# Weighted sums of four modulation rows: pairs behind fixed VectorE operations in place of bursts of eight, and a higher rank for two kinds of splits

## The chip, the cores and the metric

The kernel runs on one core of a Trainium2 chip. The metric is the device time of one execution in microseconds (us). The engines are TensorE (PE in the rows; PEld is its weight load), VectorE (DVE), ScalarE (ACT), GpSimd (POOL) and SyncE (SP), which issues most transfers. Each engine works through a queue of its own in order, and waits on semaphores for the others.

## What is computed

One layer of a diffusion backbone over 1024 latent tokens and 256 context tokens, model width 1024, all in 32-bit floats. Cut to what matters here:

```python
mod = silu(c) @ w_mod + b_mod                      # w_mod: 1024 x 6144
sh1, sc1, g1, sh2, sc2, g2 = split(mod, 6)         # six rows of 1024
hx = rmsnorm(x) * (1 + sc1) + sh1
proj = hx @ w_in                                   # u_f (512), u_x (512), u_g (512)
y_f = fft2(u_f).real                               # 4 groups of 128 channels
xc = dwconv(u_x, 4 taps)
for d in (0, 1):                                   # forward, backward
    r = sigmoid(xc @ wa[d]); i = sigmoid(xc @ wi[d])
    a = exp(-8 * r * softplus(-lam[d]))
    h = scan(a, sqrt(1 - a * a) * i * xc)
    y += h
y_r = y * gelu(u_g)
x = x + g1 * (concat(y_f, y_r) @ w_out)
hx2 = rmsnorm(x) * (1 + sc2) + sh2
out = rmsnorm(x + g2 * expert_choice_swiglu(hx2))  # 16 experts, d_ff 2816
```

The rows sh1 and sc1 are wanted at the start, and g1, sh2, sc2 and g2 only behind the mixing. The change concerns those last four.

## The kernel before

The program runs in stages. The first loads x and the context, makes sh1 and sc1, normalises and transposes (to about 75 us). `phase_c`, the mixing stage, follows up to about 270 us: the projections in tiles of 128 channels by 1024 tokens, the convolution, the gates and scans, the gelu product and the Fourier transform by matrices. `phase_f` multiplies by w_out (tiles mx) and adds the residual, to about 400 us. Then come the router and the 16 experts, up to the end.

TensorE computes in 32 bits by splitting both operands into a high and a low half and issuing three matmuls for each product (`mm3`, L611). For every weight tile ScalarE makes the high half (L227; `wh`) and VectorE the low half (L228; `wl`). The tiles of the projection are numbered ct: 0 to 3 give the Fourier input (`uf0` to `uf3`, PSUM), 4 to 7 the scan input (`ux`), 8 to 11 the gelu input (`ug0` to `ug3`). `get(ct)` loads a tile's two halves by h and calls `get_w` for both, so `wl8_0` is the low half of the first half of tile 8, which `ug0` reads. One projection is 48 matmuls of 512 columns.

For each t in 0 to 3 the stage computes: `conv(t)` (six multiply-adds, L658, tile xc), `xsplit(t)` (xch, xcl), four gate products on TensorE (`g`, 9 matmuls each; g201 is tile 2, direction 0, gate 1), sigmoids on ScalarE, the exponent and the square root there, the product with xc on VectorE (`lru_sig`, L697 to L700), `lru_scan` for each direction (two steps, L713 and L714, on tile r; the scan, L716, into tile g), the sum of both directions (L813), `gelu(t)` (product at L822, tile gg), `fourier_a(g)` (ScalarE copies the reversed half of uf to uT; VectorE makes tile U by L885 to L888). `fb_dft`, `fb_split`, `fb_trig` and `fb_evac` are the two matrix steps of the Fourier transform (tiles ab and abx, abl and xl, pq, T and yf). The projection outputs share two PSUM slots, so ug2 takes the slot of uf2 when VectorE has read it.

The weighted sums: `mod_acc(r, h)` makes half of modulation row r for all partitions. It loads w_mod in four transfers of 512 KB on GpSimd's queue (tile `mraw`, two buffers) and adds eight products of 128x512 into a tile `macc` on VectorE (L837 starts a sum, L839 adds). The tile is stored to `accd`; the matrix stage sums it over the partitions later. Eight calls of `mod_acc` are written by hand between the steps of `phase_c`.

The order on an engine is not that of the code: a scheduler sorts the instructions by priority, which follows the place in the program. `high_priority(offset=n)` moves an instruction ahead by n, and `pin` keeps an instruction behind the one traced before it on the same engine. Before, `get_w` and `fb_split` use the offset HP = 50, and `mod_acc` pins nothing.

Of the kernel before, what the change touches and what calls it, by code (L numbers as in the profile page):

```python
# [9 lines left out]
F32 = mybir.dt.float32  # L10
# [4 lines left out]
ALU = mybir.AluOpType  # L15

D = 1024
N = 1024
NCTX = 256
L = N + NCTX  # L20
KD = 8
# [138 lines left out]


class Kern:
    HP, HT, LATE = 50, 300, -100
    PAD = 32

    def __init__(self, ctx, tc, a, out, dbg=None):
# [429 lines left out]

    def get_w(self, ct, h):
        raw = self.wraw.pop((ct, h))
        with self.tc.high_priority(offset=self.HP):
            return self._get_w(ct, h, raw)  # L600

    def _get_w(self, ct, h, raw, pin=False, eng=None):
# [46 lines left out]
    def conv(self, t):  # L649
        nc = self.nc  # L650
        u = self.u.pop(t)
        xc = self.c5(f"xc{t}", tag="xc")
        col = lambda i: self.cols[:, COL["cw"] + 4 * i + t:COL["cw"] + 4 * i + t + 1]
        cb = self.cols[:, COL["cb"] + t:COL["cb"] + t + 1]
        for o, n, q in ((0, N, NCTX), (N, NCTX, 0)):
            nc.scalar.activation(xc[:, q:q + n], u[:, o:o + n], AF.Identity, scale=col(1), bias=cb)
            for i, a, b in ((0, 1, n), (2, 0, n - 1), (3, 0, n - 2)):
                nc.vector.scalar_tensor_tensor(xc[:, q + a:q + b], u[:, o + a + i - 1:o + b + i - 1], col(i),  # L658
                                               xc[:, q + a:q + b], op0=ALU.mult, op1=ALU.add)
        self.xc[t] = xc  # L660

    def xsplit(self, t):
# [47 lines left out]

    def lru_scan(self, d, r, g, a):
        V = self.nc.vector
        V.scalar_tensor_tensor(r, a, 1.0, r, op0=ALU.add, op1=ALU.mult)  # L713
        V.tensor_tensor(r, r, g, op=ALU.mult)  # L714
        s = slice(None) if d == 0 else slice(None, None, -1)
        V.tensor_tensor_scan(g[:, s], a[:, s], r[:, s], 0.0, op0=ALU.mult, op1=ALU.add)  # L716

    def phase_c(self, stop=None):
        nc = self.nc
        self.xc, self.xs, self.graw, self.gw = {}, {}, {}, {}  # L720
        self.ysp = self.dram.tile([7, 128, N], F32, name="ysp")
        self.yl = {}
        self.accd = self.dram.tile([4, 2, 128, 512], F32, name="accd")
        st = {}
        self.load_gate(0)
        self.conv(0)
        self.xsplit(0)
        self.load_trig()
        self.ux(2)
        self.gate_w(0)  # L730
        self.get(7)
        st[0] = self.lru_front(0)
        self.load_gate(1)
        self.conv(1)
        self.xsplit(1)
        self.ux(3)
        self.get(0)
        self.gate_w(1)
        self.lru_back(0, *st[0])
        self.fourier_a(0)  # L740
        self.mod_acc(0, 0)
        self.conv(2)
        self.get(8)
        self.load_gate(2)
        st[1] = self.lru_front(1)
        self.mod_acc(0, 1)
        self.xsplit(2)
        self.gelu(0)
        self.mod_acc(1, 0)
        self.gate_w(2)  # L750
        self.get(1)
        self.lru_back(1, *st[1])
        self.conv(3)
        self.fourier_a(1)
        self.mod_acc(1, 1)
        self.get(9)
        self.load_gate(3)
        st[2] = self.lru_front(2)
        self.mod_acc(2, 0)
        self.xsplit(3)  # L760
        self.gelu(1)
        self.mod_acc(2, 1)
        self.gate_w(3)
        self.get(2)
        self.lru_back(2, *st[2])
        self.fourier_a(2)
        self.mod_acc(3, 0)
        self.get(3)
        st[3] = self.lru_front(3)
        self.fourier_a(3)  # L770
        self.get(10)
        self.lru_back(3, *st[3])
        self.gelu(2)
        self.get(11)
        self.fd = {}
        self.fb_dft(0)
        self.fb_split(0)
        self.gelu(3)
        self.mod_acc(3, 1)
        if stop == "e":  # L780
            self.fd = {}
            for g in range(CT):
                self.fb_dft(g)
                self.fb_split(g)
                self.fb_trig(g)
                self.fb_evac(g)
# [21 lines left out]
    def lru_back(self, t, st, a):  # L808
        nc = self.nc
        for d in range(2):  # L810
            self.lru_scan(d, *st[d], a[d])
        g0, g1 = st[0][1], st[1][1]
        nc.vector.tensor_tensor(g0[:, NCTX:], g0[:, NCTX:], g1[:, 0:N], op=ALU.add)  # L813
        self.yl[t] = g0[:, NCTX:]

    def gelu(self, t):
        nc = self.nc
        p = self.p2(f"ug{t}")
        self.proj(p, 8 + t)
        gg = self.pr.tile([128, N], F32, tag="gg", name=f"gg{t}", bufs=1)  # L820
        nc.scalar.activation(gg, p, AF.Gelu_apprx_tanh)
        nc.vector.tensor_tensor(gg, gg, self.yl.pop(t), op=ALU.mult)  # L822
        self.dump(f"yr{t}", gg)
        nc.sync.dma_start(self.ysp[3 + t], gg)

    def mod_acc(self, r, h):
        nc, a = self.nc, self.a
        m, s = (2, 4, 3, 5)[r], slice(512 * h, 512 * h + 512)
        acc = self.pr.tile([128, 512], F32, tag="ht", name=f"macc{m}{h}", bufs=2)
        for kp in range(KD // 2):  # L830
            w = self.pro.tile([128, 2, 512], F32, tag="mraw", name=f"mraw{m}{h}{kp}", bufs=2)
            nc.gpsimd.dma_start(w, a["wmod"][m, 2 * kp:2 * kp + 2, :, s].rearrange("k p c -> p k c"))
            for i in range(2):
                k = 2 * kp + i
                c = self.cond[:, k:k + 1]
                if k == 0:
                    nc.vector.tensor_scalar(acc, w[:, i], c, None, op0=ALU.mult)  # L837
                else:
                    nc.vector.scalar_tensor_tensor(acc, w[:, i], c, acc, op0=ALU.mult, op1=ALU.add)  # L839
        nc.gpsimd.dma_start(self.accd[r, h], acc)  # L840

    def mod_row(self, r, acc, b, ones, p):
        nc = self.nc
# [32 lines left out]
    def fourier_a(self, g):  # L876
        nc = self.nc
        V = nc.vector
        p = self.p2(f"uf{g}")
        self.proj(p, g)  # L880
        U = self.c4(f"U{g}", (128, 2, 512))
        uT = self.pr.tile([128, 512], F32, tag="uT", name=f"uT{g}", bufs=1)
        nc.scalar.activation(uT, p[:, 1023:511:-1], AF.Copy)
        rev = uT[:, 0:511]
        V.tensor_tensor(U[:, 0, 1:], p[:, 1:512], rev, op=ALU.add)  # L885
        V.tensor_tensor(U[:, 1, 1:], p[:, 1:512], rev, op=ALU.subtract)
        V.tensor_copy(U[:, 0, 0:1], p[:, 0:1])
        V.tensor_copy(U[:, 1, 0:1], uT[:, 511:512])  # L888
        self.fo[g] = U
# [16 lines left out]
    def fb_split(self, g):  # L906
        p, px = self.fd[g]
        hi, lo = self.c4(f"abh{g}", (128, 8, 128), F32R), self.c4(f"abl{g}", (128, 8, 128), F32R)
        xh = self.pr.tile([1, 128], F32R, tag="xh", name=f"xh{g}", bufs=1)
        xl = self.pr.tile([1, 128], F32R, tag="xl", name=f"xl{g}", bufs=1)  # L910
        with self.tc.high_priority(offset=self.HP):
            for s in range(2):
                self.split(p[:, 512 * s:512 * s + 512].rearrange("p (a b) -> p a b", b=128),
                           hi[:, 4 * s:4 * s + 4], lo[:, 4 * s:4 * s + 4])
            self.split(px[0:1, 0:128], xh, xl)
        self.fd[g] = hi, lo, xh, xl
# [657 lines left out]
    def load(self, p):  # L1574
        if p >= len(self.order):
            return
        k, m = self.order[p]
        if k == "w":
            self.raws[m] = self.raw_tile(f"raw{m}")
            self.nc.sync.dma_start(self.raws[m], self.S[m][5])  # L1580
        else:
            src = self.accx.rearrange("(t p) c -> p t c", p=128)
            self.fin.append(self.raw_tile(f"fin{m}"))
            self.nc.sync.dma_start(self.fin[-1].rearrange("p (t c) -> p t c", t=2), src[:, 2 * m:2 * m + 2])
# [252 lines left out]
```

## Time and profile before

| what | value |
|---|---|
| median of 3 runs | 1981.69 us (1981.35 to 1982.66) |
| the profiled execution, own time | 1983.2 us |
| its span in the profile | 1981.4 us |
| TensorE busy | 1899.9 us |
| VectorE busy | 1750.4 us |
| ScalarE busy | 1357.3 us |
| accumulations | 8 of L837, 56 of L839 |
| transfers of mraw | 32, of 512 KB |

The span is the time between the first and the last recorded instruction of one execution. Busy times include the issue of neighbouring instructions that overlap by some hundredths of a us, so distances from start to start are used where a sum is made. A row of the timeline gives the start, the busy time, the engine, the line and operation, the tile written and the tiles read, and in brackets how long the engine sat idle before it and what released it.

### The profile page before, as it was taken

How to read it: one execution, taken by the hardware profiler on the slowest of the kernel's cores; microseconds unless marked ns; L12 is line 12 of the kernel's file. 1: busy time of each engine (PE TensorE's matmuls, PEld its weight loads, DVE VectorE, ACT ScalarE, POOL GpSimd, SP SyncE). 2: the span in 40 equal slices, each digit the busy share in tenths (PEclk: the TensorE clock that was granted, in tenths of full speed). 3: DMA queues.
4: the chain of work that ended last, by engine and by line, in shares of the span. 5: the costliest groups of instructions: out<-in, count | busy, mean ns of one | idle time of the engine just before them, and what ended most of it. 6: DMA issues, size and time to landing. Idle time of an engine off the chain costs nothing.

```text
span 1981.4 us, 24505 instructions
## 1 busy us (share of the span) xinstructions
PE 1899.9 (96%) x9434; PEld 1559.9 (79%) x9434; DVE 1750.4 (88%) x1629; ACT 1357.3 (69%) x1094; POOL 137.0 (7%) x134
## 2 busy tenths in 40 slices
PE   7989889969999999999999999999999999999996
PEld 2777777857787888888888888888888888888885
DVE  7889787789998989898999999998989898989897
ACT  6567643346676777777777777777777777777775
POOL 2310101220002000000000000000000000000000
PEclk9999989979999999999999999999999999999998
DMA  8353554578999999999999999999999999999994
GB/s 330 112 159 123 191 173 149 207 285 334 350 357 339 379 368 390 381 386 367 388 363 391 355 406 364 396 366 381 379 381 375 384 381 376 385 375 387 366 390 178
DMA packets 113956, 651.34 MB, mean 329 GB/s; under 512 B 12743, under 2 KB 20472, under 8 KB 46254
## 3 DMA queue, kind: packets, MB, share of 16 engines
q1 hardware_dynamic: 100718, 602.55, 79.2%
q0 software_dynamic: 10816, 38.82, 6.9%
q10 hardware_dynamic: 2304, 8.39, 1.1%
q8 instruction: 74, 1.21, 0.2%
q14 instruction: 44, 0.36, 0.0%
HBM read 622.98 MB, written 26.74 MB: 328 GB/s over the span
## 4 chain that ended last, share of the span: by engine, by line
PE 76%; DVE 9%; DMA 6%; issue 5%; ACT 1%; POOL 1%; SPq 0%; POOLq 0%; DVEq 0%; ACTq 0%
PE gu L611 44%; PE y L611 22%; PE mx L611 4%; DVE lo L228 3%; DMA mraw<-in_wmod_dram 3%; PE ht L1627 2%; DMA x<-in_x_dram 1%; DVE macc L839 1%; PE xt L1498 1%; ACT hi L227 1%; DMA trr<-in_trig_dram 1%; PE hp L1185 1%; PE pq L611 1%; DVE g L716 0%; DVE r L714 0%
## 5 line engine op out<-in xcount | busy, mean ns | idle before, releaser
L228 DVE TENSOR_TENSOR lo<-raw,hi 128x2048 fp32r<-128x2048 f32 x525 | 1197.8, 2296 | 130.2 <-ACT hi L227 128.9
L227 ACT ACTIVATE hi<-raw 128x2048 fp32r<-128x2048 f32 x525 | 1006.9, 1918 | 311.2 <-PE gu L611 210.2
L611 PE MATMUL gu<-hi,xgh 128*128 128x512 f32 (+1 forms) x1536 | 580.0, 378 | 0.0
L611 PE MATMUL gu<-hi,xgl 128*128 128x512 f32 (+1 forms) x1536 | 572.9, 373 | 0.0
L611 PE MATMUL gu<-lo,xgh 128*128 128x512 f32 (+1 forms) x1536 | 572.2, 373 | 0.0
L611 PEld LDWEIGHTS gu<-hi,xgl 128*128 128x128 f32 x1536 | 290.2, 189 | 51.8 <-DVE xgl L228 0.2
L611 PEld LDWEIGHTS gu<-lo,xgh 128*128 128x128 f32 x1536 | 290.7, 189 | 49.0 <-issue 0.2
L611 PEld LDWEIGHTS gu<-hi,xgh 128*128 128x128 f32 x1536 | 290.5, 189 | 48.6 <-issue 0.2
L611 PE MATMUL y<-hi,hh 128*128 128x512 f32 x704 | 282.3, 401 | 0.0
L611 PE MATMUL y<-hi,hl 128*128 128x512 f32 x704 | 276.2, 392 | 1.4 <-DVE hl L228 1.4
L611 PE MATMUL y<-lo,hh 128*128 128x512 f32 x704 | 275.0, 391 | 0.0
L611 PEld LDWEIGHTS y<-hi,hl 128*128 128x128 f32 x704 | 132.5, 188 | 30.7 <-DVE hl L228 1.8
L611 PEld LDWEIGHTS y<-lo,hh 128*128 128x128 f32 x704 | 132.9, 189 | 25.5 <-issue 0.2
L611 PEld LDWEIGHTS y<-hi,hh 128*128 128x128 f32 x704 | 132.8, 189 | 25.0 <-issue 0.2
L1620 ACT ACTIVATE hid<-gu 128x512 f32<-128x512 f32 x96 | 54.1, 564 | 87.1 <-PE gu L611 87.1
L1637 POOL DMA_INDIRECT accx<-ys,idx x15 | 24.0, 1598 | 1014.2 <-DVE ys L1636 940.8
L228 DVE TENSOR_TENSOR hl<-ht,hh 128x512 fp32r<-128x512 f32 x96 | 61.4, 640 | 0.0
L1621 DVE TENSOR_TENSOR hid<-hid,gu 128x512 f32<-128x512 f32 x96 | 61.0, 636 | 0.0
L1627 PE MATMUL ht<-k_ident,hid 128*128 128x128 f32 x352 | 54.7, 274 | 5.3 <-DVE hid L1621 5.3
L1627 PEld LDWEIGHTS ht<-k_ident,hid 128*128 128x128 f32 x352 | 44.1, 141 | 19.2 <-DVE hid L1621 7.3
L839 DVE SCALAR_TENSOR_TENSOR macc<-mraw,cond,macc 128x512 f32<-128x512 f32 x56 | 41.8, 748 | 18.8 <-DMA mraw<-in_wmod_dram 18.1
L227 ACT ACTIVATE hh<-ht 128x512 fp32r<-128x512 f32 x96 | 52.0, 542 | 3.5 <-PE ht L1627 3.5
(434 smaller groups left out, 1819.6 us busy)
## 6 DMA issues: line engine op xcount, KB each, us to landing
raw<-in_wg_dram SPq DMA_DIRECT2D x160, 1024.0 KB, 7.1
raw<-in_wu_dram SPq DMA_DIRECT2D x160, 1024.0 KB, 7.3
raw<-in_wd_dram SPq DMA_DIRECT2D x160, 1024.0 KB, 7.1
raw<-in_wt_dram SPq DMA_DIRECT2D x32, 1024.0 KB, 7.7
mraw<-in_wmod_dram POOLq DMA_DIRECT2D x32, 512.0 KB, 4.7
raw<-in_wdt_dram SPq DMA_DIRECT2D x16, 1024.0 KB, 6.9
wm<-in_wmod_dram SPq DMA_DIRECT2D x16, 512.0 KB, 9.7
wr<-in_win_dram SPq DMA_DIRECT2D x24, 256.0 KB, 3.5
```

The costliest lines, as they stand in the source:

```text
L227: i = self.nc.scalar.activation(hi, src, AF.Copy)
L228: j = (eng or self.nc.vector).tensor_tensor(lo, src, hi, op=ALU.subtract)
L611: i = nc.tensor.matmul(out, l, r, start=st, stop=sp)
L839: nc.vector.scalar_tensor_tensor(acc, w[:, i], c, acc, op0=ALU.mult, op1=ALU.add)
L1185: self.pin(nc.tensor.matmul(q[:, 1024:1024 + E], hT[:, k], wr[:, k], start=k == 0, stop=k == KD - 1))
L1498: nc.tensor.transpose(p[:, 128 * i:128 * i + 128], xg[:, 128 * k:128 * k + 128], self.ident)
L1620: nc.scalar.activation(hid[:, 0:w], p[:, 0, 0:w], AF.Silu)
L1621: nc.vector.tensor_tensor(hid[:, 0:w], hid[:, 0:w], p[:, 1, 0:w], op=ALU.mult)
L1627: self.nc.tensor.transpose(q[:, c:c + 128], hid[:, c:c + 128], self.ident)
L1637: self.nc.gpsimd.indirect_dma_start(out=self.accx, out_offset=bass.IndirectOffsetOnAxis(ap=idx[:, :1], axis=0), in_=ys, in_offset=None, co ...
```

## The change

Three things change. The offset of `get_w` and `fb_split` becomes HW = 150. `mod_acc` and its eight calls go, and a generator `mod_gen` takes their place: each step loads one transfer ahead and adds one pair of products; loads, products and the store are pinned. The generator is driven by `tick`, which wraps fixed VectorE instructions (convolution, scan steps, scan, sum of directions, gelu product, the two large operations of U): it pins the instruction, adds its cost to a counter, and for each 1.7 of the counter emits a pair. The counter is switched on just before `lru_back(0)`, that is before the first scan. What is left is emitted behind `gelu(3)`. The work is the same: 64 accumulations, 32 loads, 8 stores.

```diff
-    HP, HT, LATE = 50, 300, -100
+    HP, HW = 50, 150
...
     def get_w(self, ct, h):
         raw = self.wraw.pop((ct, h))
-        with self.tc.high_priority(offset=self.HP):
+        with self.tc.high_priority(offset=self.HW):
...
     def lru_scan(self, d, r, g, a):
         V = self.nc.vector
-        V.scalar_tensor_tensor(r, a, 1.0, r, op0=ALU.add, op1=ALU.mult)
-        V.tensor_tensor(r, r, g, op=ALU.mult)
+        self.tick(V.scalar_tensor_tensor(r, a, 1.0, r, op0=ALU.add, op1=ALU.mult), 1.5)
+        self.tick(V.tensor_tensor(r, r, g, op=ALU.mult), 1.5)
         s = slice(None) if d == 0 else slice(None, None, -1)
-        V.tensor_tensor_scan(g[:, s], a[:, s], r[:, s], 0.0, op0=ALU.mult, op1=ALU.add)
+        self.tick(V.tensor_tensor_scan(g[:, s], a[:, s], r[:, s], 0.0, op0=ALU.mult, op1=ALU.add), 2.8)
...
+        self.mg, self.cost = self.mod_gen(), None
         self.load_gate(0)
...
         self.gate_w(1)
+        self.cost = 0.0
         self.lru_back(0, *st[0])
         self.fourier_a(0)
-        self.mod_acc(0, 0)
         self.conv(2)
...
         self.gelu(3)
-        self.mod_acc(3, 1)
+        for _ in self.mg:
+            pass
...
+    STEP = 1.7
+
+    def tick(self, i, cost):
+        self.pin(i)
+        if self.cost is None:
+            return
+        self.cost += cost
+        while self.cost >= self.STEP:
+            self.cost -= self.STEP
+            next(self.mg, None)
+
+    def mod_gen(self):
...
+        def load(n):
+            if n < len(todo):
+                r, h, kp = todo[n]
+                m, s = (2, 4, 3, 5)[r], slice(512 * h, 512 * h + 512)
+                w[n] = self.pro.tile([128, 2, 512], F32, tag="mraw", name=f"mraw{m}{h}{kp}", bufs=2)
+                self.pin(nc.gpsimd.dma_start(w[n], a["wmod"][m, 2 * kp:2 * kp + 2, :, s].rearrange("k p c -> p k c")))
+
+        load(0)
+        for n, (r, h, kp) in enumerate(todo):
+            load(n + 1)
...
+                if k == 0:
+                    self.pin(nc.vector.tensor_scalar(acc, w[n][:, i], c, None, op0=ALU.mult))
+                else:
+                    self.pin(nc.vector.scalar_tensor_tensor(acc, w[n][:, i], c, acc, op0=ALU.mult, op1=ALU.add))
...
-        V.tensor_tensor(U[:, 0, 1:], p[:, 1:512], rev, op=ALU.add)
-        V.tensor_tensor(U[:, 1, 1:], p[:, 1:512], rev, op=ALU.subtract)
+        self.tick(V.tensor_tensor(U[:, 0, 1:], p[:, 1:512], rev, op=ALU.add), 0.7)
+        self.tick(V.tensor_tensor(U[:, 1, 1:], p[:, 1:512], rev, op=ALU.subtract), 0.7)
```

The `tick` calls around the convolution (1.3 and 0.5), the sum of directions (1.2) and the gelu product (1.2) are of the same kind. `fb_split` gets HW like `get_w`.

The lines of the changed kernel are up to 21 higher from there on. The first place is VectorE at the first scan of t=0 (r00, r01: direction 0 and 1 of t=0; g00, g01 the same for the scan's output). Before:

```order
L837 TENSOR_SCALAR macc41_1475<-mraw410_1476,cond_185 128x512
L839 SCALAR_TENSOR_TENSOR macc41_1475<-mraw410_1476,cond_185,macc41_1475 128x512
L713 SCALAR_TENSOR_TENSOR r00_983<-a00_1014,r00_983 128x1280
L713 SCALAR_TENSOR_TENSOR r01_1008<-a01_1017,r01_1008 128x1280
L228 TENSOR_TENSOR gl1_1128<-gr1_1022,gh1_1127 128x512
L714 TENSOR_TENSOR r00_983<-r00_983,g00_984 128x1280
L714 TENSOR_TENSOR r01_1008<-r01_1008,g01_1009 128x1280
L716 SCALAR_TENSOR_TENSOR g00_984<-a00_1014,r00_983 128x1280
L716 SCALAR_TENSOR_TENSOR g01_1009<-a01_1017,r01_1008 128x1280
L228 TENSOR_TENSOR wl8_0_1226<-wr8_0_1221,wh8_0_1225 128x512
L813 TENSOR_TENSOR g00_984<-g00_984,g01_1009 128x1024
L228 TENSOR_TENSOR wl8_1_1230<-wr8_1_1223,wh8_1_1229 128x512
```

and now:

```order
L714 SCALAR_TENSOR_TENSOR r00_983<-a00_1014,r00_983 128x1280
L715 TENSOR_TENSOR r00_983<-r00_983,g00_984 128x1280
L228 TENSOR_TENSOR xcl1_1034<-xc1_1024,xch1_1033 128x1280
L228 TENSOR_TENSOR wl8_0_1259<-wr8_0_1254,wh8_0_1258 128x512
L228 TENSOR_TENSOR wl8_1_1263<-wr8_1_1256,wh8_1_1262 128x512
L855 TENSOR_SCALAR macc00_1137<-mraw200_1133,cond_185 128x512
L857 SCALAR_TENSOR_TENSOR macc00_1137<-mraw200_1133,cond_185,macc00_1137 128x512
L717 SCALAR_TENSOR_TENSOR g00_984<-a00_1014,r00_983 128x1280
L857 SCALAR_TENSOR_TENSOR macc00_1137<-mraw201_1135,cond_185,macc00_1137 128x512
```

The accumulations ahead of the first scan step are gone (the last two of 26 are the first two rows of before), wl8_0 and wl8_1 stand behind the first product in place of behind both scans, and the first accumulations follow them.

The second place is VectorE ahead of the last reads of uf2, the U2 copies. Before:

```order
L713 SCALAR_TENSOR_TENSOR r21_1552<-a21_1561,r21_1552 128x1280
L837 TENSOR_SCALAR macc50_1738<-mraw500_1739,cond_185 128x512
L714 TENSOR_TENSOR r21_1552<-r21_1552,g21_1553 128x1280
L885 TENSOR_TENSOR U2_1731<-uf2_1682,uT2_1732 128x511
L716 SCALAR_TENSOR_TENSOR g21_1553<-a21_1561,r21_1552 128x1280
L886 TENSOR_TENSOR U2_1731<-uf2_1682,uT2_1732 128x511
L813 TENSOR_TENSOR g20_1528<-g20_1528,g21_1553 128x1024
L697 TENSOR_TENSOR g30_1789<-g30_1789,xc3_1410 128x1280
L887 COPY U2_1731<-uf2_1682 128x1
L888 COPY U2_1731<-uT2_1732 128x1
```

and now:

```order
L698 TENSOR_TENSOR g30_1807<-g30_1807,xc3_1443 128x1280
L857 SCALAR_TENSOR_TENSOR macc31_1702<-mraw510_1694,cond_185,macc31_1702 128x512
L717 SCALAR_TENSOR_TENSOR g21_1586<-a21_1594,r21_1585 128x1280
L857 SCALAR_TENSOR_TENSOR macc31_1702<-mraw511_1700,cond_185,macc31_1702 128x512 x2
L857 SCALAR_TENSOR_TENSOR macc31_1702<-mraw512_1706,cond_185,macc31_1702 128x512 x2
L810 TENSOR_TENSOR g20_1561<-g20_1561,g21_1586 128x1024
L906 TENSOR_TENSOR U2_1764<-uf2_1715,uT2_1765 128x511
L857 SCALAR_TENSOR_TENSOR macc31_1702<-mraw513_1710,cond_185,macc31_1702 128x512 x2
L700 TENSOR_TENSOR g31_1832<-g31_1832,xc3_1443 128x1024
L701 TENSOR_TENSOR g31_1832<-g31_1832,xc3_1443 128x256
L907 TENSOR_TENSOR U2_1764<-uf2_1715,uT2_1765 128x511
L908 COPY U2_1764<-uf2_1715 128x1
```

Before, 49 of the 64 accumulations stand ahead of the copy that reads uf2 last; now all 64 do, as do wl10, wl11 and the first wol (not in these rows), and both parts of g31.

The third place is TensorE at the end of the gates of t=3, where g301, g310 and g311 are gate products, uf3 the last Fourier projection and ug2 the third gelu projection. Before, at the last gate:

```order
L611 MATMUL g311_1803<-xch3_1584,gh3_1659 128x256
L611 MATMUL g311_1803<-xcl3_1585,gh3_1659 128x256
L611 MATMUL g311_1803<-xch3_1584,gl3_1660 128x256
L611 MATMUL uf3_1827<-hTh7_554,wh3_1_1764 128x512
L611 MATMUL uf3_1827<-hTl7_555,wh3_1_1764 128x512
L611 MATMUL uf3_1827<-hTh7_554,wl3_1_1765 128x512
L611 MATMUL ug2_1902<-hTh0_443,wh10_0_1887 128x512
L611 MATMUL ug2_1902<-hTl0_444,wh10_0_1887 128x512
```

and now:

```order
L611 MATMUL uf3_1845<-hTl7_555,wh3_1_1782 128x512
L611 MATMUL uf3_1845<-hTh7_554,wl3_1_1783 128x512
L611 MATMUL g301_1796<-xch3_1599,gh3_1661 128x512
L611 MATMUL g301_1796<-xcl3_1600,gh3_1661 128x512
...
L611 MATMUL g311_1821<-xch3_1599,gh3_1661 128x256
L611 MATMUL g311_1821<-xcl3_1600,gh3_1661 128x256
L611 MATMUL g311_1821<-xch3_1599,gl3_1662 128x256
L611 MATMUL ug2_1920<-hTh0_443,wh10_0_1905 128x512
```

Before, the gate products lie between pieces of uf3; now all of uf3 stands ahead of g301, and the gates follow each other up to ug2. The first gate product of t=3, g300, stands ahead of uf3 in both.

## Rows read from the trace of the kernel before

**Rows 1.** The page, busy time of TensorE (us, share of the span, instructions).

```profile
PE 1899.9 (96%) x9434; PEld 1559.9 (79%) x9434; DVE 1750.4 (88%) x1629; ACT 1357.3 (69%) x1094; POOL 137.0 (7%) x134
```

**Rows 2.** Stretches: length, busy time by engine, granted clock, transfer share, GB/s.

```profile
125.00:150.00 25.00, 18.20 (x72) 14.33 (x71) 21.20 (x23) 13.46 (x17) 2.89 (x5) 0.86 0.41 126
...
175.00:200.00 25.00, 23.34 (x108) 18.84 (x107) 24.03 (x30) 19.44 (x20) 3.01 (x5) 1.00 0.35 117
200.00:225.00 25.00, 19.97 (x83) 15.79 (x83) 19.29 (x19) 16.82 (x16) 3.79 (x6) 0.93 0.55 169
...
250.00:275.00 25.00, 16.96 (x98) 14.34 (x97) 23.67 (x39) 12.24 (x17) 0.56 (x1) 0.87 0.51 170
...
400.00:1981.40 1581.40, 1539.28 (x7692) 1282.21 (x7690) 1427.10 (x1030) 1135.90 (x798) 65.90 (x51) 0.99 0.96 366
```

**Rows 3.** Waits of TensorE, 130 to 275: us, times, longest.

```profile
PE ug L611 <- DVE wl L228: 8.5, 2, 6.8
PE abx L903 <- DVE xl L228: 6.4, 1, 6.4
PE uf L611 <- DVE wl L228: 5.0, 1, 5.0
```

**Rows 4.** Instructions of macc, its engine's idle time before them, landing of mraw.

```profile
L839 DVE SCALAR_TENSOR_TENSOR macc<-mraw,cond,macc x56: 728/751/754, 85.1 to 257.9; 128x512 f32<-128x512 f32 x56
...
  DMA mraw<-in_wmod_dram: 23.5, 16
...
DMA to landing us min/median/max: 4.0/4.7/7.9
```

**Rows 5.** Stretches, instructions that read or write macc alone: VectorE, GpSimd.

```profile
84.00:132.40 48.40, 18.39 (x26) 1.73 (x3) 1.00 0.53 169
132.40:227.00 94.60, 16.38 (x24) 1.73 (x3) 0.95 0.40 128
```

**Rows 6.** Waits of VectorE, 84 to 132.4 (first) and 132.4 to 268.7 (second).

```profile
DVE macc L839 <- DMA mraw<-in_wmod_dram: 6.8, 5, 2.7
...
DVE macc L839 <- DMA mraw<-in_wmod_dram: 11.3, 6, 4.1
```

**Rows 7.** Timeline of VectorE, first scans of t=0 and what follows.

```profile
132.44 2.89 DVE L713 SCALAR_TENSOR_TENSOR r<-a,r 128x1280 f32<-128x1280 f32 x2
...
138.65 5.53 DVE L716 TENSOR_TENSOR_SCAN g<-a,r 128x1280 f32<-128x1280 f32 x2
144.10 0.67 DVE L228 TENSOR_TENSOR wl<-wr,wh 128x512 fp32r<-128x512 f32 x1
```

**Rows 8.** Timeline of TensorE, the same place.

```profile
144.82 0.79 PE L611 MATMUL ug<-hTh,wl 128*128 128x512 f32 x1 [6.80 <-DVE wl L228]
```

**Rows 9.** Timeline of VectorE, from the last U2 copy to the last gg.

```profile
227.00 0.15 DVE L888 COPY U<-uT 128x1 f32<-128x1 f32 x1
227.06 0.75 DVE L839 SCALAR_TENSOR_TENSOR macc<-mraw,cond,macc 128x512 f32<-128x512 f32 x1
227.72 0.69 DVE L228 TENSOR_TENSOR wl<-wr,wh 128x512 fp32r<-128x512 f32 x1
...
267.59 1.20 DVE L822 TENSOR_TENSOR gg<-gg,g 128x1024 f32<-128x1024 f32 x1
```

**Rows 10.** Timeline of TensorE: first ug2, pq0, ab2, pq1, ab3.

```profile
229.58 0.39 PE L611 MATMUL ug<-hTh,wh 128*128 128x512 f32 x1
...
256.83 0.48 PE L611 MATMUL pq<-trig,abh 128*128 128x258 f32 x2 [0.72 <-DVE abl L228]
...
261.46 2.15 PE L900 MATMUL ab<-dft,U 128*128 128x128 f32 x16 [0.89 <-ACT gg L821]
...
270.60 0.77 PE L611 MATMUL pq<-trig,abh 128*128 128x258 f32 x2
...
276.89 2.96 PE L900 MATMUL ab<-dft,U 128*128 128x128 f32 x16
```

**Rows 11.** Timeline of ScalarE, the square roots of t=0.

```profile
127.28 2.44 ACT L805 ACTIVATE r<-r 128x1280 f32<-128x1280 f32 x2
```

More of the change, by code (lines that the diff above doesn't have):

```diff
@@ L657, in conv @@
             for i, a, b in ((0, 1, n), (2, 0, n - 1), (3, 0, n - 2)):
-                nc.vector.scalar_tensor_tensor(xc[:, q + a:q + b], u[:, o + a + i - 1:o + b + i - 1], col(i),
-                                               xc[:, q + a:q + b], op0=ALU.mult, op1=ALU.add)
+                self.tick(nc.vector.scalar_tensor_tensor(xc[:, q + a:q + b], u[:, o + a + i - 1:o + b + i - 1],
+                                                         col(i), xc[:, q + a:q + b], op0=ALU.mult, op1=ALU.add),
+                          1.3 if n == N else 0.5)
         self.xc[t] = xc
@@ L745, in phase_c @@
         st[1] = self.lru_front(1)
-        self.mod_acc(0, 1)
         self.xsplit(2)
         self.gelu(0)
-        self.mod_acc(1, 0)
         self.gate_w(2)
@@ L754, in phase_c @@
         self.fourier_a(1)
-        self.mod_acc(1, 1)
         self.get(9)
@@ L758, in phase_c @@
         st[2] = self.lru_front(2)
-        self.mod_acc(2, 0)
         self.xsplit(3)
         self.gelu(1)
-        self.mod_acc(2, 1)
         self.gate_w(3)
@@ L766, in phase_c @@
         self.fourier_a(2)
-        self.mod_acc(3, 0)
         self.get(3)
@@ L812, in lru_back @@
         g0, g1 = st[0][1], st[1][1]
-        nc.vector.tensor_tensor(g0[:, NCTX:], g0[:, NCTX:], g1[:, 0:N], op=ALU.add)
+        self.tick(nc.vector.tensor_tensor(g0[:, NCTX:], g0[:, NCTX:], g1[:, 0:N], op=ALU.add), 1.2)
         self.yl[t] = g0[:, NCTX:]
@@ L821, in gelu @@
         nc.scalar.activation(gg, p, AF.Gelu_apprx_tanh)
-        nc.vector.tensor_tensor(gg, gg, self.yl.pop(t), op=ALU.mult)
+        self.tick(nc.vector.tensor_tensor(gg, gg, self.yl.pop(t), op=ALU.mult), 1.2)
         self.dump(f"yr{t}", gg)
         nc.sync.dma_start(self.ysp[3 + t], gg)
-    def mod_acc(self, r, h):
-        nc, a = self.nc, self.a
[L828 to L832, printed above, removed]
+    STEP = 1.7
[8 more added lines that the diff above has]
+    def mod_gen(self):
+        nc, a = self.nc, self.a
+        todo = [(r, h, kp) for r in range(4) for h in range(2) for kp in range(KD // 2)]
+        w, acc = {}, {}
+        def load(n):
[7 more added lines that the diff above has]
+            load(n + 1)
+            if kp == 0:
+                acc = self.pr.tile([128, 512], F32, tag="ht", name=f"macc{r}{h}", bufs=2)
             for i in range(2):
@@ L836, in mod_acc @@
                 if k == 0:
-                    nc.vector.tensor_scalar(acc, w[:, i], c, None, op0=ALU.mult)
+                    self.pin(nc.vector.tensor_scalar(acc, w[n][:, i], c, None, op0=ALU.mult))
                 else:
-                    nc.vector.scalar_tensor_tensor(acc, w[:, i], c, acc, op0=ALU.mult, op1=ALU.add)
-        nc.gpsimd.dma_start(self.accd[r, h], acc)
+                    self.pin(nc.vector.scalar_tensor_tensor(acc, w[n][:, i], c, acc, op0=ALU.mult, op1=ALU.add))
+            del w[n]
+            if kp == KD // 2 - 1:
+                self.pin(nc.gpsimd.dma_start(self.accd[r, h], acc))
+            yield
     def mod_row(self, r, acc, b, ones, p):
@@ L910, in fb_split @@
         xl = self.pr.tile([1, 128], F32R, tag="xl", name=f"xl{g}", bufs=1)
-        with self.tc.high_priority(offset=self.HP):
+        with self.tc.high_priority(offset=self.HW):
             for s in range(2):
```

## The prediction

> **What bounds the kernel now.** I read the page first. TensorE is busy for 1899.9 of 1981.4 us [rows 1], so time is won or lost only where TensorE stands still or where its work is made to start later. The table of stretches shows where that is: TensorE has only 18.20, 19.97 and 16.96 us of 25 in three stretches of the mixing stage, and there the granted clock reads 0.86, 0.93 and 0.87 [rows 2]. VectorE is busy for 21.20, 24.03, 19.29 and 23.67 us in the same rows: in this stage it is nearly as full as TensorE. The waits of TensorE in the stage name VectorE each time: ug for wl 8.5, abx for xl 6.4, uf for wl 5.0 [rows 3]. All three are low halves of a split that stood late in VectorE's queue. So the stage has two engines that take turns in binding, and the MoE stage behind it is bound by TensorE and only slides with the stage's end.
>
> The accumulations are 64 instructions on VectorE, 0.75 us each, and VectorE sat idle in front of them for 23.5 us because their transfers had not landed; a transfer takes 4.7 us in the median, 7.9 at most [rows 4]. Now comes what decides the forecast: where they stand. 26 of the 64 run between 84 and 132.4, ahead of the first scan; 23 more (24 in the row, one of which is the 26th's tail) end before the U2 copy at 227; 15 run after it [rows 5, 9]. In the early stretch VectorE waits at least 6.8 us for data of these loads, so it has room there; behind it, up to the end of the first Fourier output, 11.3 us [rows 6]. (The rows count the 56 that add; the eight that start a sum wait 5.4 more, which with 18.1 makes the 23.5.)
>
> **The change, part by part.** *Priorities.* The two halves of wl8 stood behind both scans of t=0: the scans start at 138.65, wl8 is made at 144.10 [rows 7], and TensorE waits for it 6.80 us before its matmul at 144.82, which then takes 0.79, where 0.39 stands in a row at full clock [rows 8, 10]. Now the halves stand right behind r00*g00 and xcl1. The first scan step starts when ACT's square root of r00 is done: before, that run of two starts at 127.28, so the first is done at about 128.5 [rows 11], but three accumulations and their waits hold the step until 132.44 [rows 7]. Without them, and with ACT's copy xch1 moved behind the square roots, I put it at 128.0. Then 1.40 + 1.40 (two steps, by the x2 of 2.89 with the next row) + 1.40 (xcl1) + 0.60 puts wl8_0 at 132.8, earlier than TensorE asks for it (138.0, which is 144.82 less 6.80). The first stall, 6.8, goes, and with the slow matmuls behind it about 2 us more. So TensorE is some 7 to 9 us ahead at the second gate of t=1.
>
> *Accumulations.* None is now emitted before the scan. That removes 26 from the early stretch, where VectorE has nothing to put in their place (it waits for ACT and TensorE there), and all 64 stand between the first scan step and the U2 copy, with 15 pulled ahead of that copy. VectorE's work between these two points, in distances from start to start: before, 94.56 us (132.44 to 227.00 [rows 7, 9]), of which 9.7 are idle in the timeline between them (most of the 11.3 of rows 6 among them), so 84.8 of work. It gains 41 accumulations at 0.66 (the distance in rows 9), some 0.77 where two follow each other in one tile: 28.1. It gains wl10, wl11 and wol4, six splits at 0.60: 3.6. It gains the two parts of g31*xc: 1.5. That is 118.0 of work.
>
> So without a single wait the U2 copy comes at 128.0 + 118.0 = **246.0**, 19 us later than now. The start that is 4.4 earlier and the stalls that vanish are paid for several times over: TensorE's lead of 7 to 9 us is eaten because uf1 (waits for the U0 copy, whose PSUM slot it takes), g200 (for xcl2), g300 (for xcl3, which stands behind 45 accumulations) and ug2 (for the U2 copy) each stand behind accumulations. I expect the largest stall ahead of g300, about 12 us.
>
> *Waits for the loads.* Two buffers as before, now a load pinned ahead of each pair. 32 pairs in 118 us is a pair every 3.7; a buffer comes free two pairs earlier, so a load has about 7 us where 4.7 + 0.3 are needed. But the cost counter releases two pairs behind a scan, and there VectorE waits. Walking the order by hand with 4.4 to 5.0 for a landing, I get 7 us of such waits and 2 us for ACT; the U2 copy then comes at **255**. This is the term I know least. Lower bound: zero. Upper: the 23.5 us that all 64 cost in bursts now [rows 4], which gives 269.5.
>
> Of these waits the Trainium skill has two things to say. Under "Trainium Kernel Development and Optimization", section Best Practices, it asks to double-buffer so that transfers lie beside compute; by that the waits are nil. The trace speaks against taking it for granted: two buffers are there now and VectorE still waited 23.5 us. Under "SBUF — State Buffer", section "SBUF: two separate sides", it says that a transfer issued from GpSimd's queue can be held up while VectorE runs a copy of a kind that locks the shared port (620 ns grow to about 3100). By the trace, landings lie between 4.0 and 7.9 us, median 4.7, in a stage where VectorE is 77 to 96% busy [rows 2, 4], so at most a mild form of it is seen.
>
> *From the U2 copy to the end of the stage.* ug2 takes the PSUM slot of uf2, so it can't start before the U2 copy; before, it starts at 229.58, 2.6 behind it, TensorE being busy until then. From there to the first matmul of pq1 at 270.60 are 41.0 us [rows 10], of them 0.72 + 0.89 + 6.43 waits [rows 3, 10], so 33.0 of work. The stall of 6.4 can't recur in full, since VectorE has no accumulation left in this part: from the U2 copy to gg3 it has 22.8 us of work against 40.6 now [rows 9]. But TensorE comes to ug2 from a stall of several us and so at the lower of its two clocks for its first rows; ug3 waits for ACT's gelu of ug2, which stands behind the square roots of t=3; pq1 waits for the reads of pq0. I take 5 us for these three, so 38.2: pq1 at 255.1 + 38.2 = 293.3, against 270.6: **+22.7**. Before, pq1 ran behind a long stall and took 6.29 (270.60 to 276.89), where pq0 with the same 26 matmuls took 3.74 (256.83 to 261.46, less 0.89) [rows 10]: that gives back 2.6. So **+20**. Behind pq1 the same work follows in both, and nothing there can make up for it: 1539.28 of the last 1581.40 us are TensorE's [rows 2].
>
> *What costs nothing.* Instruction counts are the same on every engine. The splits of ab at the higher rank fall in the part where VectorE has slack. The accumulated rows are wanted only after pq2, and are stored earlier than before.
>
> The profiled execution took 1983.2 us (span 1981.4), the median of the runs is 1981.69; I add the difference to the median: **2001.7 us**.
>
> **Rivals.** *The loads are hidden* (+4 to +10). U2 copy at 246.0, tail 33.0, pq1 at 279.0: +8.4, less 2.6: +5.8, 1987.5 us. For it: 7 us per load against 5. Against it: the pairs are not evenly spaced, and TensorE's stalls cost clock. *The loads come late* (+25 to +40): each landing is nearer to 7.9 than to 4.7, waits stay at 23.5, the U2 copy is at 269.5 and the end at +34, 2016 us. For it: a fuller VectorE, one queue, a store of the sums in the same queue. Against it: the median. (The first of these two is what the Best Practices of the Trainium skill would make of the time, the second what its SBUF page would.) *No change* (within 4 us): VectorE's work from the first scan step to gg3 is 140.7 us, so gg3 could end its wait at 268.7, where it starts at 267.59 now [rows 9]; if the order of TensorE were loose enough for the U2 copy not to matter, the stage would end as before, 1982.8 us. Against it: ug2 has the one slot to take. *Faster*: the wl stalls (8.5 + 5.0) and the slow matmuls behind each (some 2 + 1) are gone, and the accumulations cost VectorE nothing that TensorE sees: 1965 us. The point that decides it is whether the U2 copy stays before 229 us; it would need the accumulations to run in half their time, or VectorE to have some 19 us of idle time where the rows show it busy for 24.03 of 25. I see neither.
>
> **How the numbers follow.** Slower by 10 to 25 us, the forecast: 0.60. Loads late, +25 to +40: 0.10. Loads hidden, +4 to +10: 0.17. No change: 0.06. Faster: 0.07. A measurement of this kernel tells about 0.2%, 4 us, from no change. So faster 0.07, same 0.06, slower 0.87. The range takes the cases of a loss, from the upper edge of no change, 1986, to near the end of late loads, 2014; about 0.83 lies in it.
>
> **What would show it.** Right: VectorE idle for 20 us or more between 95 and 128; r00 at about 128; no wait of ug0 for wl8; stalls of TensorE at uf1, g200, g300 (the largest) and ug2, all on VectorE; the U2 copy at 250 to 260; no 6.4 at abx2; pq1 at about 293; waits for mraw of 5 to 10 us. Wrong: the U2 copy before 235, or TensorE full through 150 to 255. What would make it wrong: accumulations cheaper than 0.66 when spaced apart, waits for transfers well off 7 us, or a tail that shrinks by more than the 6.4 us of abx2.

## The result, and the profile after

The changed kernel takes 2001.62 us (median of 4 runs, 1996.34 to 2002.38), the kernel before 1981.52 on the same chip (1978.75 to 1982.66): a ratio of 1.0097, interval 1.0078 to 1.0116. It is slower by 20.1 us. The forecast was 2001.7 us.

The stretches of the changed kernel, columns as in [rows 2]:

```profile
100.00:125.00 25.00, 25.00 (x139) 21.49 (x138) 10.25 (x12) 18.01 (x19) 0.00 (x0) 1.00 0.11 32
125.00:150.00 25.00, 25.00 (x115) 20.41 (x113) 21.61 (x24) 14.54 (x18) 3.40 (x5) 1.00 0.41 133
...
175.00:200.00 25.00, 18.14 (x80) 14.31 (x80) 22.85 (x22) 16.75 (x15) 5.38 (x8) 0.99 0.68 217
200.00:225.00 25.00, 16.07 (x50) 12.46 (x51) 24.23 (x35) 13.06 (x14) 4.97 (x7) 0.70 0.53 167
225.00:250.00 25.00, 15.50 (x66) 12.14 (x64) 21.27 (x22) 12.96 (x13) 5.38 (x8) 0.91 0.66 216
250.00:275.00 25.00, 20.46 (x79) 16.38 (x80) 16.33 (x20) 17.11 (x17) 1.27 (x2) 0.79 0.37 126
```

VectorE is at 10.25 of 25 us between 100 and 125, with no accumulation and 32 GB/s of transfers: the early room is unused. TensorE is now full from 125 to 150, where it had 18.20 [rows 2]: the stall for wl8 is gone. From 175 on it has 18.14, 16.07 and 15.50 us, at a clock of 0.70 in the worst stretch, while VectorE stays at 21 to 24. The lead was spent within 50 us. At the second gate of t=1 it was 8.6 us (the first row is of the changed kernel, the second of the kernel before); at the first gate of t=2 TensorE is 1.8 us behind (175.46, before 173.71):

```profile
139.44 0.50 PE L611 MATMUL g<-xch,gh 128*128 128x512 f32 x1
```

```profile
147.97 0.63 PE L611 MATMUL g<-xch,gh 128*128 128x512 f32 x1
```

The largest waits of TensorE, 120 to 310, and of VectorE, 128 to 300 (us, times, longest):

```profile
PE g L611 <- ACT r L694: 17.4, 5, 6.5
PE g L611 <- ACT xch L227: 9.6, 2, 8.0
PE ug L611 <- DVE U L908: 4.5, 1, 4.5
```

```profile
DVE macc L857 <- DMA mraw<-in_wmod_dram: 8.6, 9, 2.2
DVE r L714 <- ACT r L802: 6.1, 3, 3.2
...
DVE macc L855 <- DMA mraw<-in_wmod_dram: 1.0, 2, 0.9
```

No wait for wl or xl is left [rows 3]. New ones stand in their place, and two of these three name ScalarE. Most of that is passed on, as ScalarE's own largest waits in 130 to 260 show:

```profile
ACT r L694 <- DVE g L717: 20.0, 3, 7.1
ACT xch L227 <- DVE xc L658: 7.7, 2, 5.2
```

A sigmoid on ScalarE (L694) writes a tile that a scan on VectorE (L717) must first have read, and a gate product on TensorE needs the PSUM slot that the sigmoid reads; xch needs the convolution. So a late VectorE shows up on TensorE with ScalarE's name on it. The places themselves on TensorE and VectorE:

```profile
219.53 0.79 PE L611 MATMUL g<-xch,gh 128*128 128x512 f32 x1 [8.01 <-ACT xch L227]
...
249.84 0.79 PE L611 MATMUL g<-xch,gh 128*128 128x512 f32 x1 [6.46 <-ACT r L694]
257.95 0.80 PE L611 MATMUL ug<-hTh,wh 128*128 128x512 f32 x1 [4.54 <-DVE U L908]
```

```profile
127.14 1.49 DVE L714 SCALAR_TENSOR_TENSOR r<-a,r 128x1280 f32<-128x1280 f32 x1 [2.21 <-ACT r L802]
...
131.48 1.28 DVE L228 TENSOR_TENSOR wl<-wr,wh 128x512 fp32r<-128x512 f32 x2
...
257.75 0.15 DVE L908 COPY U<-uf 128x1 f32<-128x1 f32 x1
...
291.70 1.23 DVE L819 TENSOR_TENSOR gg<-gg,g 128x1024 f32<-128x1024 f32 x1 [0.98 <-ACT gg L818]
```

The scan step starts 5.3 us earlier than before, the U2 copy that ug2 waits for comes 30.8 later, and gg3, the start of the last gelu product, 24.1 later [rows 7, 9]. That copy (L908) is the one that reads uf2; before, it stands just ahead of the copy of [rows 9]:

```profile
226.93 0.16 DVE L887 COPY U<-uf 128x1 f32<-128x1 f32 x1
```

The rest of the program is the same: in the 116.3 us from the first mx matmul on, TensorE is busy for 115.95 us (before, 115.97).

### The profile page after: what moved, and what is told of

It reads as the page before. It is cut to its first block, busy times and chain, and to the rows that moved or that the text cites. A ratio compares the mean times of both kernels' runs of the same rounds, so it can differ in the third digit from the quotient of the medians.

```text
span 2000.6 us, 24520 instructions
## 1 busy us (share of the span) xinstructions
PE 1902.3 (95%) x9434; PEld 1559.2 (78%) x9434; DVE 1751.0 (88%) x1629; ACT 1358.4 (68%) x1094; POOL 137.7 (7%) x134
## 4 chain that ended last, share of the span: by engine, by line
PE 76%; DVE 9%; issue 6%; DMA 5%; ACT 2%; POOL 0%; SPq 0%; POOLq 0%; DVEq 0%; ACTq 0%
PE gu L611 44%; PE y L611 21%; PE mx L611 4%; DVE lo L228 4%; DMA mraw<-in_wmod_dram 2%; PE ht L1648 2%; DVE macc L857 1%; DMA wm<-in_wmod_dram 1%; PE xt L1519 1%; PE ug L611 1%; ACT hi L227 1%; DMA trr<-in_trig_dram 1%; PE hp L1206 1%; PE pq L611 0%; DMA xg<-hxd,idx 0%
## 5 line engine op out<-in xcount | busy, mean ns | idle before, releaser
L611 PEld LDWEIGHTS gu<-lo,xgh 128*128 128x128 f32 x1536 | 290.4, 189 | 50.1 <-DVE lo L228 1.2
```

The costliest lines, as they stand in the source:

```text
L611: i = nc.tensor.matmul(out, l, r, start=st, stop=sp)
```

## The experiments

Theory T is that of the prediction: the sums lose the time, since their work left a stretch where VectorE has room and now stands in one where it binds. Rival W puts the loss on the waits behind the loads, rival P on the pinned order or the rank. All runs were timed against the kernel before on their chip: 1981.43 us for e1, e2, e3 and e7, 1982.64 for e4, e5, e6 and e8, 1983.24 for e9 to e12. The last four columns are from the profiled execution: the U2 copy that reads uf2, the sums on VectorE behind it, gg3, and mx0, the start of the first mx matmul, with which the stage after this one begins.

| kernel | us | ratio, interval | U2 copy | sums behind it | gg3 | mx0 |
|---|---|---|---|---|---|---|
| before | 1981.5 | | 226.9 | 15 | 267.6 | 283.7 |
| changed | 2001.62 | 1.0097 (1.0078 to 1.0116) | 257.8 | 0 | 291.7 | 305.5 |
| e1_rank | 1984.93 | 1.0016 (1.0006 to 1.0026) | 226.4 | 16 | 270.4 | 287.0 |
| e2_pairs | 2003.27 | 1.0107 (1.0090 to 1.0124) | 260.2 | 0 | 294.1 | 307.8 |
| e3_narrow | 1991.08 | 1.0044 (1.0028 to 1.0061) | 248.7 | 0 | 282.6 | 296.3 |
| e7_noload | 1990.51 | 1.0042 (1.0025 to 1.0059) | 244.4 | 0 | 276.1 | 293.0 |
| e9_neither | 1960.65 | 0.9889 (0.9873 to 0.9906) | 218.7 | 0 | 254.7 | 265.9 |
| e10_floor | 1960.01 | 0.9887 (0.9871 to 0.9904) | 214.0 | 0 | 246.7 | 263.4 |
| e4_loose | 1993.82 | 1.0053 (1.0037 to 1.0070) | 244.9 | 11 | 280.2 | 296.2 |
| e5_early | 1999.71 | 1.0090 (1.0073 to 1.0106) | 251.7 | 0 | 290.4 | 301.9 |
| e6_step | 1992.18 | 1.0049 (1.0033 to 1.0066) | 231.9 | 19 | 277.4 | 294.6 |
| e8_both | 1995.71 | 1.0066 (1.0050 to 1.0083) | 241.5 | 12 | 280.9 | 298.0 |
| e11_pool | 2016.67 | 1.0167 (1.0150 to 1.0184) | 267.5 | 0 | 302.1 | 318.8 |
| e12_poolrank | 2026.67 | 1.0224 (1.0207 to 1.0241) | 273.8 | 0 | 312.8 | 328.7 |

**The rank alone.** In the kernel before, `get_w` and `fb_split` only:

```diff
-    HP, HT, LATE = 50, 300, -100
+    HP, HW = 50, 150
```

> The kernel before with the higher rank of the weight and Fourier splits alone; the bursts of eight stay. Theory T (the loss is VectorE's accumulations, taken out of an early stretch with room and put ahead of the U2 copy): the accumulations keep their places (26, 22 and 15 against 26, 23 and 15, one later), so nothing is lost, and TensorE's waits for wl (8.5 and 5.0) go; VectorE's work up to the U2 copy stays 84.7 us, so little of that reaches the end: 1972 to 1983 us, U2 copy at 222 to 230. Rival P (the rank or the pinning loses the time): 1990 or more.

1984.93 us, slower than before by 0.16%, where T had a gain. The waits for wl went as expected, but nothing was won: now the gates wait 9.6 us for ScalarE's r (before none), which I put down to the splits that go first and put off the scans (the first scan starts at 139.74, before at 138.65), and abx still waits 6.0 for xl. VectorE was nearly full there, so a new order only chose who waits. T was too good by 2 us at least; P, with 1990, is not borne out.

**The pairs alone.** The changed kernel with the old rank:

```diff
-    HP, HW = 50, 150
+    HP, HW = 50, 50
```

> The changed kernel with the old rank (50 in place of 150): the pairs alone. T: as slow as the changed kernel or a little slower, 1998 to 2008 us, since 64 accumulations still stand between the first scan step and the U2 copy. P (rank): 1985 or less.

2003.27 us: as T says. The loss is in the pairs and what was pinned with them, not in the rank.

**Work and waits taken apart.** First the work without the waits' places changed, 56 accumulations on one column:

```diff
-  self.pin(nc.vector.scalar_tensor_tensor(acc, w[n][:, i], c, acc, ...))
+  self.pin(nc.vector.scalar_tensor_tensor(acc[:, 0:1], w[n][:, i, 0:1], c, acc[:, 0:1], ...))
```

> The changed kernel with 56 of the 64 accumulations made on one column in place of 512 (so the sums are left out but for a column; every load, wait and place in the order stays). T: VectorE loses 56 times about 0.6 us, 33 us, ahead of the U2 copy, of which some come back as waits for loads; U2 copy at 225 to 238, 1972 to 1988 us. Rival W (waits behind the loads cost the time, not the work): waits grow by what the work loses, 1995 or more. P: 1995 or more.

1991.08 us, between T and W, and the U2 copy at 248.7 is 11 later than T's latest. The instructions and what VectorE waits for ahead of them:

```profile
L857 DVE SCALAR_TENSOR_TENSOR macc<-mraw,cond,macc x56: 194/219/222, 132.6 to 247.9; 128x1 f32<-128x1 f32 x56
...
  DMA mraw<-in_wmod_dram: 29.5, 17
```

An accumulation falls from 746 to 219 ns in the median, so 56 of them give 29.5 us; but the waits for the loads grow from 9.6 to 29.5, so VectorE gains 9.6 us on balance, and the time fell by 10.5. With less work between them the pairs only meet their loads earlier. Then the loads alone, two of them in place of 32:

```diff
-            if n < len(todo):
+            if 2 <= n < len(todo):
+                w[n] = w[n - 2]
+            elif n < 2:
...
-            del w[n]
```

> The changed kernel with two of the 32 loads only, the other pairs read those two tiles again (so the sums are of the wrong rows; the work of VectorE and its places stay). T: only the 9.6 us of waits for the loads go, and not all of them reach the end: 1991 to 1998 us. W: all of the loss goes, 1985 or less.

1990.51 us, half a microsecond below T's bound: the waits were 9.6 us and 11.1 came back. Then both, in the changed kernel and in the kernel before:

> The changed kernel with both left out: 56 accumulations on one column, and two of the 32 loads only (sums of the wrong rows). Places in the order and pins stay. Each alone gave about 11 us of the 20. Theory T2 (work and waits stand in for each other: take the work away and VectorE waits for the loads instead, take the waits away and the work stays): both together give the whole 20 us or more, 1970 to 1983 us, U2 copy at 215 to 230. Rival P (half of the loss is the pinned order or the rank): 1987 or more, U2 copy at 240 or later.

In the kernel before, the accumulations get the same one-column edit, and one load of the 32 is left:

```diff
-            w = self.pro.tile([128, 2, 512], F32, tag="mraw", ...)
-            nc.gpsimd.dma_start(w, ...)
+            if r + h + kp == 0:
+                self.mw = self.pro.tile([128, 2, 512], F32, tag="mraw", ...)
+                nc.gpsimd.dma_start(self.mw, ...)
+            w = self.mw
```

> The kernel before with the same two left out: what the sums cost there. T2: the 26 early ones cost little, the 38 in the full stretch and their 13 us of waits cost TensorE its stalls for wl and xl: 1955 to 1972 us. If VectorE does not bind before: 1977 or more.

1960.65 and 1960.01 us. The first is 9 us below T2's range: more than the loss came back. By the ratios, which set each kernel beside the kernel before on its own chip, the sums cost 1.1%, some 22 us, before, and 2.1%, some 41 us, in the changed kernel; the difference, some 19, is the loss. Without the cost of the sums the two kernels take the same time within 0.6 us, so the pins, the ranks and the fixed order lose nothing on balance once VectorE has room.

The two do not have the same order, though. Nothing in e10 pins the accumulations, and with one load to wait for all 64 ran ahead of the first scan step, where the kernel before has 26; in e9 they stayed in the full stretch, where the short ones still take 15.3 us. The instructions of macc alone, columns as in [rows 5], of e10 and under them of e9:

```profile
84.00:126.00 42.00, 11.35 (x62) 4.35 (x8) 1.00 0.25 85
126.00:220.00 94.00, 0.00 (x0) 0.00 (x0) 0.98 0.19 58
```

```profile
84.00:126.00 42.00, 0.00 (x0) 0.00 (x0) 1.00 0.15 44
126.00:220.00 94.00, 15.28 (x64) 4.38 (x8) 0.98 0.27 83
```

So e10 is the kernel before with no sum at all in the full stretch, and doesn't show what its 26 early and its 38 late sums cost one by one. That the early ones cost little is not shown either: without their full length and their waits the first scan step starts at 126.39, where it stood at 132.44.

Taken singly the work gave 10.5 and the waits 11.1 of these 41: each stands in for the other, and only both together set the stage free. That wrong sums change the work behind the stage can be left out: from mx0 to the end of the span the four kernels with wrong sums (e3, e7, e9, e10) take 1693.5 to 1696.8 us, the other ten 1693.3 to 1697.7. In e9 the gates wait 4.6 us for r, where they waited 17.4:

```profile
PE g L611 <- ACT r L694: 4.6, 3, 2.6
PE ug L611 <- DVE U L909: 1.9, 1, 1.9
```

**Fewer sums ahead of the U2 copy.** Three ways: the fixed operations not pinned (e4), a pair for each 2.4 of the counter (e6), and early pairs (e5; e8 also with 4.2):

```diff
     def tick(self, i, cost):
-        self.pin(i)
```

> The changed kernel in which the fixed VectorE operations are not pinned (only the pairs, loads and stores are). 53 accumulations stand between the first scan step and the U2 copy (64 in the changed kernel), 11 behind it; by the sum of distances VectorE's work there is 105.6 us in place of 117.9. T: U2 copy some 12 us earlier, at 244 to 248, and 1987 to 1994 us. P (the fixed order itself loses the time, not the accumulations): 1984 or less.

```diff
-    STEP = 1.7
+    STEP = 2.4
```

> The changed kernel with a pair for each 2.4 of the counter in place of 1.7: 45 accumulations between the first scan step and the U2 copy, 13 between it and gg3, 6 behind; work up to the U2 copy 102.4 us. T: the copy some 15 us earlier, the part behind it longer by 10 or more: 1985 to 1992 us. P: unchanged, 1998 or more.

```diff
         self.load_trig()
+        self.pairs(3)
         self.ux(2)
+        self.pairs(2)
...
         st[0] = self.lru_front(0)
+        self.pairs(4)
...
+        self.pairs(4)
         self.xsplit(1)
```

> The changed kernel with 13 of the 32 pairs emitted ahead of the first scan, where the bursts had them; 18 accumulations come to stand ahead of the first scan step, 46 between it and the U2 copy, work 107.4 in place of 117.9. T: 1988 to 1995 us. If the early stretch has no room after all: 2000 or more.

> Both: 13 pairs ahead of the scan and one for each 4.2 of the counter behind it. 18 accumulations ahead of the first scan step, 34 up to the U2 copy, 6 up to gg3, 6 behind; work up to the copy 100.4 us (84.7 in the kernel before). T: 1980 to 1988 us; the best of the four here.

e4, 1993.82 us, lies in T's range; without the pins a weight split is late again (uf waits 9.9 us for wl). e6, 1992.18, 0.2 above it. e6 teaches most: the U2 copy comes at 231.9, 26 us earlier than in the changed kernel, and the time falls by only 9.4. Nineteen sums now stand behind the copy, six of them behind gg3 (277.4), and the stage ends only when VectorE is through with most of them. TensorE stands 7.9 us ahead of a pq; the wait bears the name of a high half on ScalarE, but ScalarE itself had waited 7.4 us for abl, a low half that VectorE made behind five of the last six sums and a wait for a load:

```profile
PE g L611 <- ACT r L694: 8.1, 3, 5.6
PE pq L611 <- ACT yth L227: 7.9, 1, 7.9
```

```profile
285.40 0.75 DVE L857 SCALAR_TENSOR_TENSOR macc<-mraw,cond,macc 128x512 f32<-128x512 f32 x1 [2.68 <-DMA mraw<-in_wmod_dram]
286.07 0.68 DVE L228 TENSOR_TENSOR abl<-ab,abh 128x512 fp32r<-128x512 f32 x1
```

```profile
286.79 0.60 ACT L227 ACTIVATE abh<-ab 128x512 fp32r<-128x512 f32 x1 [7.38 <-DVE abl L228]
```

e5, 1999.71 us, misses its range and lies 0.3 below the mark for an early stretch without room. I take it for no clean test of that room: 18 accumulations came to stand ahead of the first scan step, as expected, but 23 more crowd in behind it, so 41 stand ahead of the U0 copy (15 in the changed kernel, 26 before) and the first scan starts at 154.20 in place of 133.87:

```profile
152.74 1.54 DVE L865 SCALAR_TENSOR_TENSOR macc<-mraw,cond,macc 128x512 f32<-128x512 f32 x2 [2.22 <-DMA mraw<-in_wmod_dram]
154.20 2.82 DVE L717 TENSOR_TENSOR_SCAN g<-a,r 128x1280 f32<-128x1280 f32 x1
```

e8 has the same crowd with 32 ahead of the U0 copy, and 1995.71 us, 8 above its range.

**Sums on another engine.** In the kernel before, the four calls with h = 1 go to GpSimd, as a product in place and a sum; then the same with the rank of e1:

```diff
+                if h == 1:
+                    G = nc.gpsimd
+                    G.tensor_scalar(acc if k == 0 else w[:, i], w[:, i], c, None, op0=ALU.mult)
+                    if k:
+                        G.tensor_tensor(acc, acc, w[:, i], op=ALU.add)
+                elif k == 0:
```

> The kernel before with half of the accumulations (the four calls with h = 1) on GpSimd, each as a product in place and a sum. VectorE loses 32 of 64, some 21 us. T2: the waits of TensorE for wl and xl shrink, 1967 to 1977 us. If it is the waits for loads and not VectorE's work: the loads still come through one queue, 1980 or more.

> The same with the higher rank of the weight and Fourier splits. T2: with VectorE less full the rank no longer puts off the scans: 1964 to 1976 us, at least as fast as the one without the rank. P: slower than the one without by 3 or more.

2016.67 and 2026.67 us: slower than the kernel before on their chip by 33 and 43, both far outside what I expected. The rank costs 10.0 us here, and P's mark of 3 or more is met. So the rank is not harmless: alone it lost 3.5 us in e1, while between e2 and the changed kernel it made no difference clear of the noise. In e11 VectorE's sums wait 47.9 us for loads (84 to 330):

```profile
DVE macc L842 <- DMA mraw<-in_wmod_dram: 34.5, 3, 15.2
DVE macc L844 <- DMA mraw<-in_wmod_dram: 13.4, 6, 3.3
```

And its other work gets slower. The groups of VectorE, 84 to 300, of e11, and under them of the kernel before:

```profile
L658 DVE SCALAR_TENSOR_TENSOR xc<-u,k_cols,xc 128x1023 f32<-128x1023 f32 (+3 forms) x24 | 26.5, 1132 | 2.7 <-ACT xc L656 2.7
...
L228 DVE TENSOR_TENSOR wl<-wr,wh 128x512 fp32r<-128x512 f32 x19 | 18.1, 972 | 0.9 <-ACT wh L227 0.9
...
L842 DVE TENSOR_SCALAR macc<-mraw,cond 128x512 f32<-128x512 f32 x4 | 3.0, 746 | 34.5 <-DMA mraw<-in_wmod_dram 34.5
```

```profile
L658 DVE SCALAR_TENSOR_TENSOR xc<-u,k_cols,xc 128x1023 f32<-128x1023 f32 (+3 forms) x24 | 20.3, 877 | 0.2 <-ACT xc L656 0.2
...
L228 DVE TENSOR_TENSOR wl<-wr,wh 128x512 fp32r<-128x512 f32 x19 | 12.9, 684 | 0.9 <-issue 0.9
```

The loads are issued from GpSimd's own queue, where they now stand behind products and sums; the landing itself is no slower (median 4.5 us, 4.7 before). I had counted what VectorE loses and not what stands in GpSimd's queue. Which share of the 33 us is the waits and which the slower VectorE was not tested. No version that makes the full sums was faster than the kernel before.

## Why the prediction was right

*The first scan step and wl8.* Forecast 128.0 and 132.8 for the first half; measured 127.14 and, for both halves, a start at 131.48. The 6.8 us of TensorE at ug0 went, and TensorE was 8.6 us ahead at the second gate of t=1, forecast 7 to 9.

*Work between the first step and the U2 copy.* 118.0 us of work and 9 of waits, copy at 255. Measured 130.6 us between the two (127.14 to 257.75). VectorE is idle for 13.6 of them, 9.6 of it for loads, which leaves 117.0 of work: the work was right, and the waits, which I had walked out as 7 for the loads and 2 for ScalarE, were 4.6 short. The step came 0.9 early and the copy 2.7 late.

*Which stalls pay for it.* I expected stalls at uf1, g200, g300 and ug2, all on VectorE, the largest, about 12 us, at g300 on xcl3. The four are there: uf1 1.26, g200 1.55, g300 8.0, which is the largest single wait and ends on xch3 first, 0.73 more on xcl3, and ug2 behind the U2 copy 4.54. Those of g200 and g300 bear ScalarE's name, not VectorE's. What I named too weakly are the gates that wait for ScalarE's r, 17.4 us in five waits, the largest entry of all: I had the scans late, but put the price on uf1, g200 and g300. The forecast did not depend on this split, since it went by VectorE's work up to the copy.

*The tail.* 38.2 us from the U2 copy to pq1; measured 37.4 (257.75 to 295.12). The 2.6 us that a pq1 at full clock gives back are there too: pq1 to mx0 takes 10.35 us (295.12 to 305.47), before it was 13.10 (270.60 to 283.70). At mx0 the kernel is 21.8 us late, at the end of the span 19.2; the MoE part of that execution is 2.6 us shorter, which I can't lay to the change, since runs of the kernel before lie up to 5.8 us apart on one chip (1978.91 to 1984.73). The mechanism held, but that the median meets the forecast within 0.1 us is luck: the copy came 2.7 late, the tail was 0.8 short and the later part 2.6 shorter, and single runs lie 6 us apart (1996.34 to 2002.38).

*The rivals.* Loads hidden: 1987.5 forecast with the copy at 246.0, 1990.51 and 244.4 by e7. The rival was sound within 3 us, and its condition, no wait at all, isn't met in the changed kernel. Loads late: landings went down, not up (the last row of [rows 4], now):

```profile
DMA to landing us min/median/max: 3.9/4.3/6.1
```

So nothing held them up further, although VectorE is as full. The rule of the Trainium skill ("SBUF — State Buffer", section "SBUF: two separate sides") is about a transfer issued from GpSimd's queue while VectorE runs an operation of a 2-port mode, such as a copy. VectorE's copies in this stage are one column wide (0.15 us), and almost all the rest reads two tensors, so no run here tests that rule, and late loads did not follow from it. And two buffers with a load ahead did not hide the transfers: 9.6 us of waits were left, worth 11.1. The double buffer that the Trainium skill asks for ("Trainium Kernel Development and Optimization", section Best Practices) hid a part of them only.

*What the prediction did not see.* It told the loss as one path, the U2 copy and then a tail, and made the tail up to mx0 some 8.0 us shorter than before (43.6 less 38.2, and 2.6); 9.1 it was. The path holds in every kernel: from mx0 to the end of the span all fourteen take 1693.3 to 1697.7 us, so mx0 sets the time. But the copy alone does not set mx0: e6 moves the copy by 26 us and wins 9. From the U2 copy to mx0 it takes 47.2 to 50.2 us in the seven kernels with no sum behind the copy and none on GpSimd, and it grows with the sums behind it: 51.3 us with 11 (e4), 56.5 with 12 (e8), 56.8 with 15 (before), 60.6 with 16 (e1), 62.7 with 19 (e6). So a sum moved past the copy makes the copy earlier and the tail longer: in e6 the copy came 25.8 earlier than in the changed kernel, the tail is 15.0 longer, and mx0 is 10.9 earlier. This is read from the table, not from an edit made for it. gg3 is a rougher sign: e9 and e10 take the same time with gg3 8 us apart.

That the early room was lost was argued from the rows; e5 and e8 put only 18 back and with them a crowd behind the scan step, so how much a clean return of all 26 would give wasn't shown. The kernel before, with the 26 in their old place, is the nearest case.

## What to carry to other kernels

Before spreading a filler through a stage, find the engine that sets the stage's end and add up its work from the stage's first step to its last; filler that leaves a stretch with room is paid for where the engine is full, however evenly it is spread: here the sums, 45.6 us of work and 9.6 of waits, cost some 41 us of time, where they had cost some 22. A stall that names a late low half was not cured by rank in an engine that was nearly full: rank only chose who waits, as the 8.5 and 5.0 us that became 9.6 show. A wait that names an engine is followed on to what that engine itself waits for. And when a cost is made of work and of waits for loads, taking one away brings the other out: take both away, in both kernels, to learn what it costs.

## What the runs showed of the hardware

With products and sums on GpSimd, the same VectorE instructions took longer: the 128x512 split 972 ns in the mean for 684, the convolution 1132 for 877, while GpSimd's 128x512 sum took 1.46 us in the median and its product for a new sum 2.77. An accumulation of one column still takes 219 ns, against 746 for 512: a good quarter of its time stays with hardly any columns.
